# Weight tiles of 2048 columns in place of 1024, each split by one copy and one subtract

## The chip, the cores and the metric

The kernel runs on one core of a Trainium2 chip. The time is the device time of one execution in microseconds (us). Engines: TensorE (PE, with its weight load PEld) multiplies, VectorE (DVE) and ScalarE (ACT) work on tiles elementwise, GpSimd (POOL) does small helpers, SyncE (SP) issues most DMA transfers from DRAM.

## The reference

The program is a two-layer network on x of 256 tokens by 1024 features, all in float32. Each layer is: a feed-forward block, a mixer (short convolution, a gated recurrence, pooling), a cross attention to 256 memory rows, and a second feed-forward block; each is followed by a residual and a layer norm.

```python
def swiglu(x, w_gate, w_up, w_down):
    return (jax.nn.silu(x @ w_gate) * (x @ w_up)) @ w_down
# ffn1_gate, ffn1_up: (DEPTH, 1024, 2816); ffn1_down: (DEPTH, 2816, 1024); ffn2 alike
# w_in: (DEPTH, 1024, D_IN); w_out, ca_q, ca_k, ca_v, ca_o: (DEPTH, 1024, 1024)
```

Every weight is used by one product per layer, so all weights stream from DRAM once: 216 MB in one execution.

## The kernel before, in words

**Products in parts.** A float32 factor is written as the sum of two rounded parts, high and low (type fp32r). `split(hi, lo, src)` (lines 60 to 62) makes them: ScalarE copies src into hi (line 61, shown as CAST `whi<-raw` for weights), and VectorE subtracts hi from src into lo (line 62, `wlo<-raw,whi`). A product is then three matmuls: high by high, high by low and low by high (`mm_rows`, lines 129 to 132, all through line 105).

**Weight tiles.** `load` (lines 64 to 93) brings a weight matrix in steps of 128 partitions by 2048 float32 numbers. Each step is two tiles of 1024 columns: two `raw` tiles filled by one DMA of 512 KB each, two `whi` and two `wlo` tiles, and two calls of `split`. The pool holds 6 `raw`, 8 `whi` and 8 `wlo` buffers, which are handed out in turn. A buffer can be filled again when the last reader of the tile in it is done. At the start, the very first weights come with `fine=True` in pieces of 512 columns. `Weights.at(k, cols)` finds the high and low slices of a block k.

**Feed-forward.** `ffn` (from line 400) walks over six column chunks of gate and up (five of 512 and one of 256). The chunk `first` makes gate and up products of its own; the middle ones are either `hidden`, which multiplies the whole gate chunk and then the whole up chunk, or `by_seven` (lines 568 to 652). Each chunk's activations are turned by DMA and VectorE (`turn`), and the down products of a chunk (`both`, tags `dn`, two slabs of 2048 columns) follow one or two chunks later. In layer 0's first ffn only chunk 4 goes by seven products; in the other three ffns chunks 2 and 4 do, so there are seven such chunks in all.

**by_seven.** Four blocks of weights (gate and up, upper and lower half of the features) are called w00, w01, w10 and w11. Instead of eight block products it makes seven, in this order: w00, w00+w01, w00+w11, w01+w11, w11, w10, w00+w10. The sums are made on VectorE in place (line 597). Each block is two tiles of 1024 columns: w00 in buffers spare0 and spare1, w01 in the buffers of the layer norm's parameters (lng, lnb), w11 in two `raw` buffers, w10 in spare2 and one `raw` buffer. Partial products lie in `sg` and `half` tiles (line 619).

**Order.** Apart from the program's first chunk, whose order is written by hand (line 494), a scheduler sets the order of instructions on each engine from the program's order, buffers and dependencies. Each engine then runs its own list strictly in order. The weight loads are issued on SP's queue.

**Other users.** `keys`, `values`, `mixer` and the attention call `load` for their weights in the same buffers; `finish` (line 303) does the layer norms and, in between, transposes h into xT (line 172), which again go through `split`.

Of the kernel before, what the change touches and what calls it, by code (L numbers as in the profile page):

```python
# [8 lines left out]
F32 = mybir.dt.float32  # L9
F32R = mybir.dt.float32r  # L10
U8 = mybir.dt.uint8
AF = mybir.ActivationFunctionType
ALU = mybir.AluOpType
# [4 lines left out]
P = 128  # L18
DEPTH = 2
SEQ = 256  # L20
DM = 1024
# [7 lines left out]
CHUNK = 512  # L29
# [17 lines left out]
def model(ctx: ExitStack, tc: tile.TileContext, t: dict, out: bass.AP):  # L47
    nc = tc.nc
    cst = ctx.enter_context(tc.tile_pool(name="cst", bufs=1))
    wp = ctx.enter_context(tc.tile_pool(name="wp", bufs=1))  # L50
# [9 lines left out]
    def split(hi, lo, src):  # L60
        nc.scalar.copy(hi, src)  # L61
        lows.append(nc.vector.tensor_tensor(lo, src, hi.bitcast(F32), op=ALU.subtract))  # L62

    def load(src, k0, nk, c0, ncol, fine=False):


        hi, lo, todo = [], [], []
        step = 2048 // ncol
        for a in range(k0, k0 + nk, step):
            half = step // 2  # L70
            raw = [
                wp.tile([P, 1024], F32, tag="raw", name="raw", bufs=6).rearrange("p (k c) -> p k c", c=ncol)
                for _ in range(2)
            ]
            part = 1 if fine else half
            for b in range(0, step, part):
                loads.append(nc.sync.dma_start(
                    raw[b // half][:, b % half : b % half + part, :],
                    src[(a + b) * P : (a + b + part) * P, c0 : c0 + ncol].rearrange("(k p) c -> p k c", p=P),
                ))  # L80
            for s in range(2):
                h = wp.tile([P, 1024], F32R, tag="whi", name="whi", bufs=8)
                w = wp.tile([P, 1024], F32R, tag="wlo", name="wlo", bufs=8)
                h = h.rearrange("p (k c) -> p k c", c=ncol)
                w = w.rearrange("p (k c) -> p k c", c=ncol)
                r = raw[s]
                if fine:
                    todo += [(h[:, b, :], w[:, b, :], r[:, b, :]) for b in range(half)]
                else:
                    split(h, w, r)  # L90
                hi.append(h)
                lo.append(w)
        return Weights(hi, lo, half, todo)

# [47 lines left out]
    h = [cst.tile([P, DM], F32, name=f"h{i}") for i in range(NT)]  # L144
# [36 lines left out]


    def load_memory(mp, behind):
        m = [
            mp.tile([P, DM], F32, tag=f"spare{n}", name="m", bufs=1).rearrange("p (k b j) -> p k b j", k=4, j=32)
            for n in range(2)
        ]
        with tc.issue_after(behind.ins):
            for n in range(2):
                for a in range(4):  # L190
                    for k in range(4):
                        c = (4 * n + k) * P + a * 32
                        nc.gpsimd.dma_start(
                            m[n][a * 32 : a * 32 + 32, k],
                            t["mem"][0, :, c : c + 32].rearrange("(b i) j -> i b j", i=32),
                        )

        def later():
            for n in range(2):
                for k in range(0, 4, 2):  # L200
                    turned = mp.tile([P, 2, SEQ], F32, tag="up", name="turned")
                    nc.vector.transpose(
                        turned.rearrange("p k t -> p (k t)"), m[n][:, k : k + 2].rearrange("p k b j -> p (k b j)")
                    )
                    d = slice(4 * n + k, 4 * n + k + 2)
                    split(mTh[:, d, :], mTl[:, d, :], turned)

        return later
# [82 lines left out]


    def ln_params(l, n):
        g = wp.tile([P, DM], F32, tag="lng", name="lng")
        b = wp.tile([P, DM], F32, tag="lnb", name="lnb")
        nc.sync.dma_start(g, t["ln_g"][l, n : n + 1, :].to_broadcast([P, DM]))
        nc.sync.dma_start(b, t["ln_b"][l, n : n + 1, :].to_broadcast([P, DM]))
        return g, b
# [101 lines left out]
    def ffn(l, name, n, pend=None, last=False, early=None):  # L400
        gate, up, down = (t[f"{name}_{x}"][l] for x in ("gate", "up", "down"))
        with tc.tile_pool(name="ffn", bufs=2, reuse_waits="tile") as fp:
# [19 lines left out]
            def activations():  # L422
                return fp.tile([P, NT, CHUNK], F32, tag="sg", name="sg", bufs=1)
# [142 lines left out]
                return parts  # L566

            def by_seven(c0, bx):
                def rows_by_columns(r):
                    return r.rearrange("p (k c) -> p k c", c=CHUNK)  # L570

                def pieces(*tags):
                    return [
                        rows_by_columns(
                            (fp if "spare" in g else wp).tile([P, DM], F32, tag=g, name="raw", bufs=6 if g == "raw" else 1)
                        )
                        for g in tags
                    ]

                def block(m, j, to):  # L580
                    for i in range(2):
                        k = 4 * j + 2 * i
                        loads.append(nc.sync.dma_start(
                            to[i], m[k * P : (k + 2) * P, c0 : c0 + CHUNK].rearrange("(k p) c -> p k c", p=P)
                        ))
                    return to

                w00 = block(gate, 0, pieces("spare0", "spare1"))
                w01 = block(up, 0, pieces("lng", "lnb"))
                w11 = block(up, 1, pieces("raw", "raw"))  # L590
                w10 = block(gate, 1, pieces("spare2", "raw"))

                def parts_of(r, plus=None):
                    hi, lo = [], []
                    for i in range(2):
                        if plus is not None:
                            nc.vector.tensor_tensor(r[i], r[i], plus[i], op=ALU.add)  # L597
                        h = wp.tile([P, 1024], F32R, tag="whi", name="whi", bufs=8)
                        w = wp.tile([P, 1024], F32R, tag="wlo", name="wlo", bufs=8)
                        h, w = (rows_by_columns(x) for x in (h, w))  # L600
                        split(h, w, r[i])
                        hi.append(h)
                        lo.append(w)
                    return Weights(hi, lo, 2, [])

                def part_of_x(i, j):
                    d = slice(4 * j, 4 * j + 4)
# [7 lines left out]
                def half_sum():  # L615
                    return fp.tile([P, 4, P], F32, tag="up", name="half").rearrange("p k t -> p (k t)")
# [4 lines left out]
                s = activations()  # L621
                g = [s[:, i, :] for i in range(NT)]
# [9 lines left out]
                f = half_sum()  # L632
# [47 lines left out]
            bx = []  # L680

            if early is None:
                d = [fp.tile([P, DM], F32, tag=f"spare{n}", name="quarters", bufs=1) for n in range(2)]
            else:
                d = [wp.tile([P, DM], F32, tag=g, name="quarters") for g in ("lng", "lnb")]
            q = [d[n // 2].rearrange("p (n k t) -> p n k t", n=2, t=P)[:, n % 2] for n in range(4)]

            chunks = [(c, min(CHUNK, DFF - c)) for c in range(0, DFF, CHUNK)]

# [22 lines left out]
            for c, (c0, ncol) in enumerate(chunks):  # L712
                if not c:
                    acts.append(first())
                    ys = [[acc((P, 512), "dn") for _ in range(2)] for _ in range(NT)]
                elif c in sevens:
                    left = by_seven(c0, bx)
                else:
                    if c in (1, 2) and early is not None:
                        acts.append(hidden(c0, aside))  # L720
                    else:
                        acts.append(hidden(c0) if ncol == CHUNK else last_hidden(c0))
                if c == 1 and early is None:
                    bx.extend(blocks_of_x())
                if c == max(sevens) + 1:
                    gb = ln_params(l, n)
                if c == 1 and early is not None:

                    with tc.issue_after(loads[-1].ins):
                        rest = early(fp)  # L730
                if c == 2 and early is not None:
                    with tc.issue_after(lows[-1].ins):
                        rest[0]()
                if c > 0:
                    if c > 1:
                        both(c - 2, 1)
                    if c in sevens:
                        acts.append(left())
                    if c < len(chunks) - 1:
                        both(c - 1, 0)  # L740
# [442 lines left out]
    def beginnings(op):  # L1183
        parameters, made = small_parameters(op)
        return parameters, load_memory(op, made)
# [35 lines left out]
```

## Time and profile before

| what | value |
|---|---|
| median of 3 runs | 1070.54 us (1070.43 to 1071.01) |
| span of the profiled execution | 1068.8 us |
| PE busy | 1059.3 us, 99% |
| PEld busy | 937.7 us, 88% |
| DVE busy, instructions | 946.3 us, 89%, 1318 |
| ACT busy, instructions | 642.4 us, 60%, 916 |
| read from HBM | 216.15 MB |

The span runs from the first to the last instruction of the profiled execution; the profile gives the execution no other time of its own, and the median of the runs is 1.7 us above the span. Busy time of an engine leaves out register, branch and DMA-issuing instructions. The busy shares are averages over the whole span. The granted TensorE clock was 0.998 of full speed over the span. Rows of instruction groups read: line, engine, operation, output<-inputs, shapes, count, then busy us and mean ns of one, then the idle time of the engine before them and what ended it. Rows of single instructions read: start in us from the span's start, length, engine, line, operation, tiles, count in a row, and in brackets the idle time before it.

### The profile page before, as it was taken

The numbers are of one execution on the slowest core, as the hardware profiler recorded it, in microseconds if no ns is written. First come the engines' busy times: TensorE is split into PE (matmuls) and PEld (weight loads), VectorE is DVE, ScalarE is ACT, GpSimd is POOL, SyncE is SP. The second block draws the span as 40 slices with busy tenths as digits, with TensorE's granted clock in tenths as the row PEclk, the third lists the DMA queues.
The fourth block names the chain that finished last, engine by engine and source line by source line (L and its number), as shares of the span: only waits on it lengthen the run. The fifth ranks groups of instructions, "written<-read, shape, count | busy, mean of one in ns | idle before, by whom it ended". The sixth has DMA issues, their size and how long they took to land.

```text
span 1068.8 us, 16312 instructions
## 1 busy us (share of the span) xinstructions
PE 1059.3 (99%) x5966; PEld 937.7 (88%) x5966; DVE 946.3 (89%) x1318; ACT 642.4 (60%) x916; POOL 66.4 (6%) x114
## 2 busy tenths in 40 slices
PE   9999999999999999999999999999999999999997
PEld 7888888889899888888888888888898998888886
DVE  6977997998988799999799999788989787999996
ACT  7555664666557565656575557566764665656660
POOL 9700001000000000000000000010000000000000
PEclk9999999999999999999999999999999999999999
DMA  9997484755574575848675865856536665759461
GB/s 362 262 307 256 129 288 165 249 176 174 170 278 167 178 252 194 290 167 218 238 272 184 256 254 183 290 179 216 196 126 213 241 227 181 257 156 334 134 223 40
DMA packets 130895, 231.90 MB, mean 217 GB/s; under 512 B 9408, under 2 KB 48608, under 8 KB 130816
## 3 DMA queue, kind: packets, MB, share of 16 engines
q1 hardware_dynamic: 129024, 228.49, 64.8%
q0 software_dynamic: 1216, 1.20, 0.5%
q8 instruction: 47, 0.77, 0.3%
q10 hardware_dynamic: 576, 1.18, 0.3%
q14 instruction: 32, 0.26, 0.1%
HBM read 216.15 MB, written 1.05 MB: 203 GB/s over the span
## 4 chain that ended last, share of the span: by engine, by line
PE 99%; DMA 0%; DVE 0%; issue 0%; DVEq 0%
PE acc L105 65%; PE dn L105 31%; PE acc L172 1%; PE dn L923 1%; PE dn L982 0%; DMA h<-in_x_dram 0%; PE acc L491 0%; PE dn L981 0%; PE dn L971 0%; PE acc L1047 0%; PE dn L888 0%; DVE h L358 0%; DVE h L353 0%; PE dn L472 0%; DVE st L338 0%
## 5 line engine op out<-in xcount | busy, mean ns | idle before, releaser
L61 ACT CAST whi<-raw 128x1024 fp32r<-128x1024 f32 (+1 forms) x438 | 442.9, 1042 | 197.5 <-DVE raw L597 54.9
L62 DVE TENSOR_TENSOR wlo<-raw,whi 128x1024 fp32r<-128x1024 f32 (+1 forms) x438 | 515.7, 1209 | 32.6 <-ACT whi L61 29.0
L105 PE MATMUL acc<-whi,xT 128*128 128x512 f32 x1032 | 312.9, 380 | 0.0
L105 PEld LDWEIGHTS acc<-whi,xT 128*128 128x128 f32 x1032 | 195.1, 189 | 27.5
L105 PE MATMUL acc<-wlo,xT 128*128 128x512 f32 x516 | 195.6, 379 | 0.0
L105 PE MATMUL acc<-xT,whi 128*128 128x512 f32 x576 | 142.3, 383 | 0.2
L105 PE MATMUL dn<-whi,ah 128*128 128x512 f32 x346 | 131.5, 380 | 0.0
L105 PE MATMUL dn<-wlo,ah 128*128 128x512 f32 x346 | 131.2, 379 | 0.0
L105 PE MATMUL dn<-whi,al 128*128 128x512 f32 x346 | 131.2, 379 | 0.0
L105 PEld LDWEIGHTS acc<-xT,whi 128*128 128x128 f32 x576 | 104.0, 190 | 12.5 <-ACT whi L61 0.7
L105 PEld LDWEIGHTS acc<-wlo,xT 128*128 128x128 f32 x516 | 97.5, 189 | 13.8
L105 PE MATMUL dn<-whi,xT 128*128 128x512 f32 x288 | 87.9, 381 | 0.0
L105 PEld LDWEIGHTS acc<-xT,wlo 128*128 128x128 f32 x576 | 75.5, 191 | 3.9
L105 PE MATMUL acc<-xT,wlo 128*128 128x256 f32 x576 | 75.9, 275 | 0.0
L105 PEld LDWEIGHTS dn<-whi,al 128*128 128x128 f32 x346 | 65.4, 189 | 9.2
L105 PEld LDWEIGHTS dn<-wlo,ah 128*128 128x128 f32 x346 | 65.4, 189 | 9.2
L105 PEld LDWEIGHTS dn<-whi,ah 128*128 128x128 f32 x346 | 65.4, 189 | 9.1
L350 POOL TENSOR_TENSOR rs<-rs,nhalf 128x1 f32<-128x1 f32 x16 | 14.9, 930 | 833.6 <-DVE rs L346 598.1
L597 DVE TENSOR_TENSOR raw<-raw 128x1024 f32<-128x1024 f32 x56 | 66.2, 1217 | 0.4
L105 PEld LDWEIGHTS dn<-whi,xT 128*128 128x128 f32 x288 | 54.4, 189 | 7.7 <-DVE xT L62 0.3
L105 PE MATMUL dn<-wlo,xT 128*128 128x512 f32 x144 | 54.6, 379 | 0.0
L332 DVE SCALAR_TENSOR_TENSOR h<-h,dn 128x512 f32<-128x512 f32 x31 | 21.2, 683 | 32.9 <-PE dn L105 32.9
(234 smaller groups left out, 1277.5 us busy)
## 6 DMA issues: line engine op xcount, KB each, us to landing
raw<-in_ffn_up_dram SPq DMA_DIRECT2D x88, 512.0 KB, 5.3
raw<-in_ffn_down_dram SPq DMA_DIRECT2D x88, 512.0 KB, 6.6
raw<-in_ffn_gate_dram SPq DMA_DIRECT2D x84, 512.0 KB, 5.1
raw<-in_w_in_dram SPq DMA_DIRECT2D x48, 512.0 KB, 4.7
dealt<-sg SPq DMA_DIRECT2D x80, 128.0 KB, 4.7
raw<-in_ca_k_dram SPq DMA_DIRECT2D x16, 512.0 KB, 4.9
raw<-in_w_out_dram SPq DMA_DIRECT2D x16, 512.0 KB, 4.5
raw<-in_ca_v_dram SPq DMA_DIRECT2D x16, 512.0 KB, 5.3
```

Source lines behind the costliest of these rows:

```text
L61: nc.scalar.copy(hi, src)
L62: lows.append(nc.vector.tensor_tensor(lo, src, hi.bitcast(F32), op=ALU.subtract))
L105: nc.tensor.matmul(o, w, x, start=start, stop=stop)
L172: nc.tensor.transpose(pt[:, k, :], src[:, (4 * j + k) * P : (4 * j + k + 1) * P], unit)
L332: nc.vector.scalar_tensor_tensor(v, v, ALPHA / scale, sums(y[i][n]), op0=ALU.mult, op1=ALU.add, accum_out=None if junk is None else st[:, ...
L350: nc.gpsimd.tensor_tensor(rs, rs, nhalf[:, 0:1], op=ALU.pow)
L597: nc.vector.tensor_tensor(r[i], r[i], plus[i], op=ALU.add)
L923: nc.tensor.matmul(o[g, hh, :], kc[:, hh, g], x, start=True, stop=True)
```

## The change

A tile of weights is 2048 columns wide: `raw` has 3 buffers in place of 6, `whi` and `wlo` 4 in place of 8, which are the same bytes. `load` calls `split` once per tile in place of twice, so one ScalarE copy and one VectorE subtract treat 128x2048 numbers. The loads themselves stay 512 KB each, two per tile. In `by_seven`, w00, w11 and w10 taken alone are split by one instruction pair as well; the sums stay additions of 1024 columns and splits of 1024 columns, but both additions now stand ahead of both splits, and the high and low tiles are one 2048 buffer each. w10 takes a whole `raw` buffer, so spare2 isn't used for it; spare0 and spare1 become one tile, as do lng and lnb.

```diff
+    def wide(kind, tag, n, ncol):
+        return wp.tile([P, 2048], kind, tag=tag, name=tag, bufs=n).rearrange("p (k c) -> p k c", c=ncol)
+
     def load(src, k0, nk, c0, ncol, fine=False):
         hi, lo, todo = [], [], []
         step = 2048 // ncol
         for a in range(k0, k0 + nk, step):
-            half = step // 2
-            raw = [
-                wp.tile([P, 1024], F32, tag="raw", name="raw", bufs=6).rearrange("p (k c) -> p k c", c=ncol)
-                for _ in range(2)
-            ]
-            part = 1 if fine else half
+            r = wide(F32, "raw", 3, ncol)
+            part = 1 if fine else step // 2
             for b in range(0, step, part):
                 loads.append(nc.sync.dma_start(
-                    raw[b // half][:, b % half : b % half + part, :],
+                    r[:, b : b + part, :],
                     src[(a + b) * P : (a + b + part) * P, c0 : c0 + ncol].rearrange("(k p) c -> p k c", p=P),
                 ))
-            for s in range(2):
-                h = wp.tile([P, 1024], F32R, tag="whi", name="whi", bufs=8)
-                w = wp.tile([P, 1024], F32R, tag="wlo", name="wlo", bufs=8)
...
-                    split(h, w, r)
-                hi.append(h)
-                lo.append(w)
-        return Weights(hi, lo, half, todo)
+            h, w = wide(F32R, "whi", 4, ncol), wide(F32R, "wlo", 4, ncol)
+            if fine:
+                todo += [(h[:, b, :], w[:, b, :], r[:, b, :]) for b in range(step)]
+            else:
+                split(h, w, r)
+            hi.append(h)
+            lo.append(w)
+        return Weights(hi, lo, step, todo)
...
     def ln_params(l, n):
-        g = wp.tile([P, DM], F32, tag="lng", name="lng")
-        b = wp.tile([P, DM], F32, tag="lnb", name="lnb")
+        both = wp.tile([P, 2, DM], F32, tag="ln", name="ln")
+        g, b = both[:, 0, :], both[:, 1, :]
...
-                w00 = block(gate, 0, pieces("spare0", "spare1"))
-                w01 = block(up, 0, pieces("lng", "lnb"))
-                w11 = block(up, 1, pieces("raw", "raw"))
-                w10 = block(gate, 1, pieces("spare2", "raw"))
+                w00 = block(gate, 0, fp, "spare")
+                w01 = block(up, 0, wp, "ln")
+                w11 = block(up, 1, wp, "raw", 3)
+                w10 = block(gate, 1, wp, "raw", 3)
 
                 def parts_of(r, plus=None):
-                    hi, lo = [], []
-                    for i in range(2):
-                        if plus is not None:
-                            nc.vector.tensor_tensor(r[i], r[i], plus[i], op=ALU.add)
-                        h = wp.tile([P, 1024], F32R, tag="whi", name="whi", bufs=8)
-                        w = wp.tile([P, 1024], F32R, tag="wlo", name="wlo", bufs=8)
-                        h, w = (rows_by_columns(x) for x in (h, w))
-                        split(h, w, r[i])
-                        hi.append(h)
-                        lo.append(w)
-                    return Weights(hi, lo, 2, [])
+                    h, w = wide(F32R, "whi", 4, CHUNK), wide(F32R, "wlo", 4, CHUNK)
+                    if plus is None:
+                        split(h, w, r)
+                    else:
+                        pairs = [slice(0, 2), slice(2, 4)]
+                        for k in pairs:
+                            nc.vector.tensor_tensor(r[:, k], r[:, k], plus[:, k], op=ALU.add)
+                        for k in pairs:
+                            split(h[:, k], w[:, k], r[:, k])
+                    return Weights([h], [w], 4, [])
```

The remaining lines of the diff rename the buffers in `load_memory` and in the tiles called quarters accordingly.

More of the change, by code (lines that the diff above doesn't have):

```diff
@@ L69, in load @@
         for a in range(k0, k0 + nk, step):
-            half = step // 2
-            raw = [
-                wp.tile([P, 1024], F32, tag="raw", name="raw", bufs=6).rearrange("p (k c) -> p k c", c=ncol)
-                for _ in range(2)
-            ]
-            part = 1 if fine else half
+            r = wide(F32, "raw", 3, ncol)
+            part = 1 if fine else step // 2
             for b in range(0, step, part):
                 loads.append(nc.sync.dma_start(
-                    raw[b // half][:, b % half : b % half + part, :],
+                    r[:, b : b + part, :],
                     src[(a + b) * P : (a + b + part) * P, c0 : c0 + ncol].rearrange("(k p) c -> p k c", p=P),
                 ))
-            for s in range(2):
-                h = wp.tile([P, 1024], F32R, tag="whi", name="whi", bufs=8)
-                w = wp.tile([P, 1024], F32R, tag="wlo", name="wlo", bufs=8)
[L84 to L89, printed above, removed]
-                    split(h, w, r)
-                hi.append(h)
-                lo.append(w)
-        return Weights(hi, lo, half, todo)
+            h, w = wide(F32R, "whi", 4, ncol), wide(F32R, "wlo", 4, ncol)
[6 more added lines that the diff above has]
+        return Weights(hi, lo, step, todo)
     def halves(a):
@@ L183, in load_memory @@
     def load_memory(mp, behind):
[L184 to L187, printed above, removed]
+        m = mp.tile([P, 2 * DM], F32, tag="spare", name="m", bufs=1)
+        m = m.rearrange("p (n k b j) -> p n k b j", n=2, k=4, j=32)
         with tc.issue_after(behind.ins):
@@ L193, in load_memory @@
                         nc.gpsimd.dma_start(
-                            m[n][a * 32 : a * 32 + 32, k],
+                            m[a * 32 : a * 32 + 32, n, k],
                             t["mem"][0, :, c : c + 32].rearrange("(b i) j -> i b j", i=32),
@@ L202, in later @@
                     nc.vector.transpose(
-                        turned.rearrange("p k t -> p (k t)"), m[n][:, k : k + 2].rearrange("p k b j -> p (k b j)")
+                        turned.rearrange("p k t -> p (k t)"), m[:, n, k : k + 2].rearrange("p k b j -> p (k b j)")
                     )
@@ L568, in by_seven, with block @@
             def by_seven(c0, bx):
[L569 to L580, printed above, removed]
+                def block(m, j, pool, tag, n=1):
+                    to = pool.tile([P, 2048], F32, tag=tag, name="raw", bufs=n).rearrange("p (k c) -> p k c", c=CHUNK)
                     for i in range(2):
@@ L583, in block @@
                         loads.append(nc.sync.dma_start(
-                            to[i], m[k * P : (k + 2) * P, c0 : c0 + CHUNK].rearrange("(k p) c -> p k c", p=P)
-                        ))
-                    return to
-                w00 = block(gate, 0, pieces("spare0", "spare1"))
-                w01 = block(up, 0, pieces("lng", "lnb"))
-                w11 = block(up, 1, pieces("raw", "raw"))
-                w10 = block(gate, 1, pieces("spare2", "raw"))
+                            to[:, 2 * i : 2 * i + 2, :],
+                            m[k * P : (k + 2) * P, c0 : c0 + CHUNK].rearrange("(k p) c -> p k c", p=P),
+                        ))
+                    return to
+                w00 = block(gate, 0, fp, "spare")
+                w01 = block(up, 0, wp, "ln")
+                w11 = block(up, 1, wp, "raw", 3)
+                w10 = block(gate, 1, wp, "raw", 3)
                 def parts_of(r, plus=None):
-                    hi, lo = [], []
-                    for i in range(2):
-                        if plus is not None:
-                            nc.vector.tensor_tensor(r[i], r[i], plus[i], op=ALU.add)
-                        h = wp.tile([P, 1024], F32R, tag="whi", name="whi", bufs=8)
-                        w = wp.tile([P, 1024], F32R, tag="wlo", name="wlo", bufs=8)
-                        h, w = (rows_by_columns(x) for x in (h, w))
-                        split(h, w, r[i])
-                        hi.append(h)
-                        lo.append(w)
-                    return Weights(hi, lo, 2, [])
+                    h, w = wide(F32R, "whi", 4, CHUNK), wide(F32R, "wlo", 4, CHUNK)
[8 more added lines that the diff above has]
+                    return Weights([h], [w], 4, [])
                 def part_of_x(i, j):
@@ L682, in ffn @@
             if early is None:
-                d = [fp.tile([P, DM], F32, tag=f"spare{n}", name="quarters", bufs=1) for n in range(2)]
+                d = fp.tile([P, 2 * DM], F32, tag="spare", name="quarters", bufs=1)
             else:
-                d = [wp.tile([P, DM], F32, tag=g, name="quarters") for g in ("lng", "lnb")]
-            q = [d[n // 2].rearrange("p (n k t) -> p n k t", n=2, t=P)[:, n % 2] for n in range(4)]
+                d = wp.tile([P, 2, DM], F32, tag="ln", name="quarters").rearrange("p n c -> p (n c)")
+            d = d.rearrange("p (n k t) -> p n k t", n=4, t=P)
+            q = [d[:, n] for n in range(4)]
             chunks = [(c, min(CHUNK, DFF - c)) for c in range(0, DFF, CHUNK)]
```

## The prediction

> **What bounds the kernel now.** I read the page first, then the chain that ended last, the groups with each shape apart, windows of single stages, and single instructions. The page's head, busy rows, clock and shares of the chain:
>
> ```profile
> span 1068.8 us, 16312 instructions
> ...
> PE 1059.3 (99%) x5966; PEld 937.7 (88%) x5966; DVE 946.3 (89%) x1318; ACT 642.4 (60%) x916; POOL 66.4 (6%) x114
> ...
> PEclk9999999999999999999999999999999999999999
> ...
> PE 99%; DMA 0%; DVE 0%; issue 0%; DVEq 0%
> PE acc L105 65%; PE dn L105 31%; PE acc L172 1%; PE dn L923 1%; PE dn L982 0%; DMA h<-in_x_dram 0%; PE acc L491 0%; PE dn L981 0%; PE dn L971 0%; PE acc L1047 0%; PE dn L888 0%; DVE h L358 0%; DVE h L353 0%; PE dn L472 0%; DVE st L338 0%
> ```
>
> TensorE sets the time. It is idle 1068.8 - 1059.3 = 9.5 us, and the chain runs through it for 99%. Two pieces of the chain in order of time (start, length, matmuls):
>
> ```profile
> 18.18 31.08 PE acc L105 x144
> 54.44 20.72 PE acc L105 x96
> ```
>
> 31.08 / 144 and 20.72 / 96 are both 216 ns a matmul: long runs without any stall. So a change that leaves the matmuls alone can win next to nothing; it can lose wherever a weight tile comes late. Whether one does hangs on VectorE, shown by two windows (length; then busy us and instructions of PE, PEld, DVE, ACT):
>
> ```profile
> 98.00:140.00 42.00, 42.00 (x196) 36.80 (x195) 40.95 (x45) 25.33 (x27) 0.00 (x0) 1.00 0.46 149
> ...
> 412.00:433.00 21.00, 21.00 (x99) 18.36 (x98) 21.00 (x25) 12.53 (x14) 0.00 (x0) 1.00 0.59 168
> ```
>
> Around a chunk done by seven products (by_seven) VectorE is as full as TensorE: 40.95 of 42 and 21.00 of 21 us. A delay there isn't made up.
>
> **Price of one instruction.** Groups with shapes apart (busy, mean ns; idle before and who ended it), ScalarE, then VectorE:
>
> ```profile
> L61 ACT CAST whi<-raw 128x1024 fp32r<-128x1024 f32 x430 | 438.2, 1049 | 197.2 <-DVE raw L597 54.9 <-PE dn L105 53.5 <-PE acc L105 35.5
> ...
> L61 ACT CAST whi<-raw 128x512 fp32r<-128x512 f32 x8 | 4.7, 624 | 0.3 <-DMA raw<-in_ffn_gate_dram 0.3
> ```
>
> ```profile
> L62 DVE TENSOR_TENSOR wlo<-raw,whi 128x1024 fp32r<-128x1024 f32 x430 | 510.4, 1219 | 32.5 <-ACT whi L61 29.0 <-PE acc L105 1.9
> ...
> L62 DVE TENSOR_TENSOR wlo<-raw,whi 128x512 fp32r<-128x512 f32 x8 | 5.4, 709 | 0.1
> ```
>
> 512 more columns cost 425 ns of copy and 510 ns of subtract, so I estimate 1049 + 850 = 1.90 us and 1219 + 1020 = 2.24 us for 2048 columns. Two subtracts back to back start 1.13 us apart (row at 425.98 below: 2.35 - 1.22), copies 0.95 us (row at 430.18: six spacings in 6.74 - 1.05); a merged pair thus occupies about 2.15 and 1.80 us in place of 2.26 and 1.90. The built program has 187 fewer instructions on each engine: 187 x 0.11 = 21 us saved on VectorE, 187 x 0.10 = 19 us on ScalarE, all beside TensorE.
>
> **The change part by part.** Matmuls, loads (number, size, queue), blockwise adds and bytes of buffers stay: nothing by themselves; if their cover went, it would show in the terms below.
>
> What costs is the grain. A 2048 buffer is free only when the readers of both its halves are done, so the copy into it starts one half later; and VectorE, which had its first half after 1.05 us of copy, waits 1.90.
>
> (a) *Start.* Row of ScalarE: a half of the first up tile comes at 14.03; below it TensorE's first low product of that tile.
>
> ```profile
> 14.03 1.04 ACT L61 CAST whi<-raw 128x1024 fp32r<-128x1024 f32 x1 [0.16 <-DMA raw<-in_ffn_up_dram]
> ```
>
> ```profile
> 18.23 0.38 PE L105 MATMUL acc<-wlo,xT 128*128 128x512 f32 x1
> ```
>
> Merged: 14.03 + 1.90 + 2.24 = 18.17 against 18.23. I take 0.1 (0 to 1.1, one subtract spacing).
>
> (b) *First by_seven of layer 0.* Copies of w00 now wait for both halves of an up tile:
>
> ```profile
> 98.67 1.05 ACT L61 CAST whi<-raw 128x1024 fp32r<-128x1024 f32 x1 [0.69 <-PE acc L105]
> 101.26 1.05 ACT L61 CAST whi<-raw 128x1024 fp32r<-128x1024 f32 x1 [1.54 <-PE acc L105]
> ```
>
> ```profile
> 132.36 1.21 DVE L62 TENSOR_TENSOR wlo<-raw,whi 128x1024 fp32r<-128x1024 f32 x1
> ```
>
> ```profile
> 134.89 0.38 PE L105 MATMUL dn<-wlo,ah 128*128 128x512 f32 x1
> ```
>
> The first copy moves from 98.67 to 101.26, 2.59 us later, and lasts 0.85 us longer, so VectorE falls 3.4 us behind in a full stage. The down tile behind the seven products ends at 133.57 with both halves; as one tile it is needed at 134.89, a reserve of 1.3. 3.4 - 1.3 = 2.1, less 0.1 saved on merges: 2.0 (0 to 3.4).
>
> (c) *First chunk of the three later ffns.* In the built order one product of the up tile stands three places into the chunk, where its neighbours are still gate products.
>
> ```profile
> 364.46 0.38 PE L105 MATMUL dn<-whi,xT 128*128 128x512 f32 x1
> ...
> 368.57 0.59 PE L105 MATMUL acc<-whi,xT 128*128 128x512 f32 x2
> ```
>
> ```profile
> 366.18 1.06 ACT L61 CAST xT<-acc 128x512 fp32r<-128x512 f32 x2
> 367.13 3.89 ACT L61 CAST whi<-raw 128x1024 fp32r<-128x1024 f32 x4
> ```
>
> The buffer of the last gate tile comes free whole at 364.7: its copy until 366.7, two copies for xT (0.95), then the up tile until 369.6, with TensorE there at 368.57: 1.0 each (0 to 1.9, the whole copy), 3.0. Everything behind it on the queue waits too; the transposes of h1 ahead of it do not.
>
> (d) *The second chunk's by_seven in the same three ffns.* VectorE, then ScalarE, then TensorE's low products of the last run, (w00+w10), and of the down tile behind it:
>
> ```profile
> 425.98 2.35 DVE L62 TENSOR_TENSOR wlo<-raw,whi 128x1024 fp32r<-128x1024 f32 x2
> ...
> 431.27 3.50 DVE L62 TENSOR_TENSOR wlo<-raw,whi 128x1024 fp32r<-128x1024 f32 x3
> ```
>
> ```profile
> 430.18 6.74 ACT L61 CAST whi<-raw 128x1024 fp32r<-128x1024 f32 x7 [5.42 <-DVE raw L597]
> ```
>
> ```profile
> 431.39 0.38 PE L105 MATMUL acc<-wlo,xT 128*128 128x512 f32 x1
> ...
> 432.69 0.38 PE L105 MATMUL acc<-wlo,xT 128*128 128x512 f32 x1
> ...
> 433.98 0.38 PE L105 MATMUL dn<-wlo,ah 128*128 128x512 f32 x1
> ```
>
> Before, the second low half ends at 431.27 + 1.22 = 432.49, 0.20 us ahead of its use. After, both adds stand ahead of the first low half, so that one ends at 432.4 and is needed at 431.39: 1.0 late. Then the order is the down tile (2.15, to 434.6) and the second half (to 435.7), while TensorE has ten down products moved between the halves. It reaches their first low product 1.3 + 0.2 us after the late start, at 433.9; 0.8 more, and with the second half hidden behind the ten, 2.0 with the switch. I add 0.8 for VectorE's late entry by mechanism (b) (bounds 0 and 3.4, nearer 0 because transposes and subtracts fill that wait here): 2.8 each (0.8 to 5.4), 8.4.
>
> (e) *The fifth chunk's by_seven in these ffns* has the reserve of (b), but keeps some earlier work ahead: 1.1 each (0 to 2.0), 3.3.
>
> (f) *Six entries of mixer, its column blocks and attention* (three a layer) start with a new tile. One such place:
>
> ```profile
> 189.10 2.35 DVE L62 TENSOR_TENSOR wlo<-raw,whi 128x1024 fp32r<-128x1024 f32 x2
> ```
>
> ```profile
> 190.32 1.05 PE L105 MATMUL acc<-xT,wlo 128*128 128x256 f32 x8
> ```
>
> A low half ends at 190.32, inside the run that reads its tile. I take 0.5 each between 0 and one subtract spacing, 1.13: 3.0 (0 to 6.8).
>
> Sum: 0.1 + 2.0 + 3.0 + 8.4 + 3.3 + 3.0 = 19.8 us of stalls. The profiled span is 1068.8 and the median 1070.54, 1.7 outside the span: 1068.8 + 19.8 + 1.7 = 1090.3, say 1090.
>
> The Trainium skill, "Perfetto Trace Analysis", section "Optimizing Scalar/DVE Operations", sets two rules side by side: larger operations improve throughput if the engine is saturated, and where Scalar and Vector aren't saturated but cause bubbles elsewhere, smaller instructions let work complete sooner. By the second the sum stands; by the first it would be near 1070. The trace has VectorE saturated in the seven-product stages and not over the span, so both speak here.
>
> **Rivals.** *No change, 1070.5.* The 21 us that VectorE saves pay for the late grain, and each tile is still there in time. For it: no wait of TensorE shows before, and most tiles have microseconds of reserve. Against: savings of 0.11 us a pair come spread out, while a reserve of 0.20 us meets a delay of 1 to 2.
>
> *Faster, 1069 to 1070.* Larger operations relieve the saturated VectorE, and TensorE's small bubbles go. It decides if part of the 9.5 us idle are waits for low tiles. Against: runs at 216 ns a matmul, and 0% of the chain on VectorE; at most 1.5 us. This is the first rule of that page of the Trainium skill ("Perfetto Trace Analysis", same section) at work.
>
> *Slower still, 1103.* w11 and w10 now hold two of three raw buffers during a by_seven, where before they held three of six halves; the next slab's load starts only when w11's last subtract is done. Seven stages late by a load's order, taken as another 1.9 us each (one copy), add 13: 1090 + 13. For it: VectorE full at 412 to 433; against: the third buffer still takes the next down tile early.
>
> **How the numbers follow.** About 0.2% (2.1 us) is what a measurement of this kernel can tell from none. Forecast 0.65, slower still 0.20, no change 0.12, faster 0.03. The likeliest is 1090, its own range 1078 to 1098: terms (b) to (f) at half, and at 1.4 times. For 8 in 10 the range goes from 1073 (just above the no-change case, which with the faster one holds 0.15) to 1105 (which takes in the slower one). Slower by over 0.2%: 0.65 + 0.20 = 0.85; within: 0.12; faster: 0.03.
>
> **What would show it.** Right: VectorE's wlo<-raw,whi with 128x2048 at 2.2 us and ScalarE's at 1.9; busy of both down by some 20 us; TensorE idle up from 9.5 to about 29, in gaps of 1 to 3 us at the places of (b) to (f), ended by L62 or L61; matmuls elsewhere still 216 ns. Wrong: runs unbroken at those places (no change), gaps ended by a load from DRAM (slower still), or a 2048 instruction that costs more than twice a 1024 one.

## Result and profile after

The changed kernel takes 1109.09 us in the median (1108.23 to 1109.99) against 1070.76 us for the kernel before: a ratio of 1.036, 95% interval 1.034 to 1.037, or 38.3 us more. Forecast were 1090 us and a range up to 1105. The direction was right; the size was half of what came.

The head of the page after, with the shares of the chain that ended last:

```profile
span 1107.6 us, 15623 instructions
...
PE 1072.7 (97%) x5966; PEld 936.8 (85%) x5966; DVE 933.8 (84%) x1131; ACT 619.3 (56%) x729; POOL 62.4 (6%) x114
...
PE 49%; DVE 28%; issue 9%; ACT 8%; DMA 6%; SPq 1%; DVEq 0%; ACTq 0%
```

The matmuls are the same 5966, and VectorE and ScalarE have 187 instructions fewer each, but the chain now runs through TensorE for only 49% of the span: 28% of it is VectorE, 8% ScalarE, 6% loads. The page's PE busy rises from 1059.3 to 1072.7 us for the same matmuls, since their ends are modelled in the profile, so stalls are better read from the starts. Groups with shapes apart:

```profile
L62 DVE TENSOR_TENSOR wlo<-raw,whi 128x2048 fp32r<-128x2048 f32 x187 | 426.5, 2287 | 98.1 <-ACT whi L61 97.3
L61 ACT CAST whi<-raw 128x2048 fp32r<-128x2048 f32 x187 | 354.0, 1908 | 139.8 <-DMA raw<-in_ffn_up_dram 30.0 <-PE dn L99 23.9 <-DMA raw<-in_ffn_gate_dram 19.6
```

One instruction costs what was estimated: 2.29 us (2.24) and 1.91 us (1.90). VectorE's busy time fell by 12.5 us (21 were estimated), ScalarE's by 23.1 (19). But VectorE now waits 97.3 us for ScalarE's long copies, where it waited 29.0 before, and ScalarE's copies wait 67.6 us for the three weight matrices of the feed-forward (30.0, 20.1 and 17.5), where it was 38.5 before (13.6, 4.6 and 20.3).

For every pair of neighbouring matmuls I took the time between their starts beyond the median of that shape, and added it up by place, over the kernel before (us; the stages are cut at the same matmuls; "three" or "two" are the number of places; the prediction's second and fifth chunk are the kernel's chunks 2 and 4, counted from 0). A table column comes from one profiled execution; e1's was 1.5 us above its median.

| place | changed | halves on wide tiles (e1) | only raw wide (e9) | only high/low wide (e10) | forecast |
|---|---|---|---|---|---|
| start (to 18 us) | 1.8 | 0.3 | 1.0 | 0.5 | 0.1 |
| first by_seven and its down products | 2.4 | 1.7 | 0.1 | -0.1 | 2.0 |
| mixer, two | 5.2 | 1.8 | 0.0 | 2.3 | with next |
| attention, two | 7.0 | 0.9 | 0.0 | 0.9 | 3.0 |
| first chunk, three | 4.1 | 0.7 | 0.0 | 0.7 | 3.0 |
| second chunk's by_seven, three | 12.7 | 12.9 | 3.1 | 4.7 | 8.4 |
| fifth chunk's by_seven, three | 5.3 | 4.1 | 0.0 | 0.7 | 3.3 |
| everything | 38.8 | 22.0 | 4.1 | 9.3 | 19.8 |

The first row can hardly be an effect of the change: the kernels of this study start with 2.7 to 4.7 us of such time in no order, and two versions below with the same instructions at the start (e2, e14) have 2.8 and 2.9, as the kernel before has. What sets it isn't shown.

### The profile page after: what moved, and what is told of

Read it like the earlier page. It is cut to its first block, busy times and chain, and to the rows that moved or that the text cites. A ratio compares the mean times of both kernels' runs of the same rounds, so it can differ in the third digit from the quotient of the medians.

```text
span 1107.6 us, 15623 instructions
## 1 busy us (share of the span) xinstructions
PE 1072.7 (97%) x5966; PEld 936.8 (85%) x5966; DVE 933.8 (84%) x1131; ACT 619.3 (56%) x729; POOL 62.4 (6%) x114
## 3 DMA queue, kind: packets, MB, share of 16 engines
HBM read 216.15 MB, written 1.05 MB: 196 GB/s over the span
## 4 chain that ended last, share of the span: by engine, by line
PE 49%; DVE 28%; issue 9%; ACT 8%; DMA 6%; SPq 1%; DVEq 0%; ACTq 0%
PE acc L99 27%; PE dn L99 19%; DVE wlo L62 15%; ACT whi L61 6%; DVE raw L583 4%; DMA raw<-in_ffn_down_dram 2%; DMA raw<-in_ffn_up_dram 1%; DVE half L601 1%; DVE sg L432 1%; DMA raw<-in_ca_q_dram 1%; DVE square L445 1%; DMA dealt<-sg 1%; PE acc L166 1%; DVE sg L601 1%; DVE sums L120 1%
## 5 line engine op out<-in xcount | busy, mean ns | idle before, releaser
L62 DVE TENSOR_TENSOR wlo<-raw,whi 128x2048 fp32r<-128x2048 f32 (+2 forms) x251 | 497.2, 1997 | 98.4 <-ACT whi L61 97.6
L61 ACT CAST whi<-raw 128x2048 fp32r<-128x2048 f32 (+2 forms) x251 | 415.0, 1675 | 247.8 <-DVE raw L583 98.7
L99 PE MATMUL dn<-whi,ah 128*128 128x512 f32 x346 | 129.0, 382 | 6.8 <-ACT whi L61 6.8
L99 PEld LDWEIGHTS dn<-whi,ah 128*128 128x128 f32 x346 | 64.9, 189 | 17.5 <-ACT whi L61 8.9
L99 PE MATMUL acc<-wlo,kTh 128*128 128x512 f32 x112 | 42.7, 381 | 0.2
```

What stands on the lines that cost most here:

```text
L99: nc.tensor.matmul(o, w, x, start=start, stop=stop)
```

## Two causes: grain of the buffers, length of the instructions

Two theories stood against each other. *Grain*: a wide buffer is free only when both halves have been read, so copies and loads start late, whatever the size of the instructions. *Length*: a 1.9 us copy and a 2.3 us subtract bring the low part late and hold up what is queued behind them. The first runs tell them apart.

**e1: wide tiles, instructions of 1024 columns.**

```diff
-                split(h, w, r)
+                for b in range(0, step, step // 2):
+                    split(*(v[:, b : b + step // 2, :] for v in (h, w, r)))
```

and in by_seven each half is added and split in turn.

> Tiles of 2048 columns as in the changed kernel, but every split is made of two copies and two subtracts of 1024 columns, and in by_seven an addition stands ahead of its own split, as before the change. Theory G (grain: a buffer of 2048 columns is free only when all of it has been read, so copies and loads start late): most of the 38 us stay, 1095 to 1109 us, with TensorE gaps still ended by L61. Theory L (length: a copy of 1.9 us and a subtract of 2.2 us bring the low part late and hold up what is queued behind them): nearly all goes, 1071 to 1077 us, gaps of TensorE as before the change.

Measured: 1091.15 us, ratio 1.018 (1.016 to 1.020). Neither theory has it all: 20.2 of the 38.3 us stay with the wide tiles alone, 18 go with the long instructions. Of the 20.2, some 4.5 come from matmuls at half clock (427 ns apart in place of 216; last section), which the changed kernel, with a granted clock of 0.998 to 0.999, doesn't have behind its stalls. For the changed kernel itself I therefore estimate 16 us for the tiles and 22 for the length.

**e9: as e1, with high and low tiles narrow again (8 of 1024); e10: the kernel before, with only high and low tiles wide (4 of 2048).**

```diff
-            h, w = wide(F32R, "whi", 4, ncol), wide(F32R, "wlo", 4, ncol)
...
+            for b in range(0, step, half):
+                h, w = narrow("whi", ncol), narrow("wlo", ncol)
...
```

> As e1_halves, but the high and low tiles are 8 of 1024 columns again; only the raw tiles are 2048 wide, 3 in all, and w10 takes a whole one. Theory R (of the grain only the raw buffers count: loads wait for a whole tile's subtract and come late): the same time as e1_halves within 4 us. Theory G with the high and low tiles as its place: within 3 us of 1070.8. Theory L: within 3 us of 1070.8 too, and e1_halves with it.

> The kernel before with high and low tiles of 2048 columns, 4 each, filled by instructions of 1024 columns; raw tiles stay 6 of 1024. Theory R: within 3 us of 1070.8. Theory G with the high and low tiles as its place: the same as e1_halves within 4 us. Theory L: within 3 us of 1070.8.

Measured: e9 1074.25 us, ratio 1.003 (1.002 to 1.004), so 3.3 us; e10 1079.29 us, ratio 1.008 (1.006 to 1.009), so 8.3 us. Theory R falls as a sole cause, and so does one place alone: 3.3 + 8.3 = 11.6, and both together 20.2. About half of this surplus of 8.6 is e1's half clock.

**e2: the changed kernel with by_seven alone in halves; e3: e1 with by_seven alone whole.**

```diff
-                    if plus is None:
-                        split(h, w, r)
-                    else:
-                        pairs = [slice(0, 2), slice(2, 4)]
-                        for k in pairs:
-                            nc.vector.tensor_tensor(r[:, k], r[:, k], plus[:, k], op=ALU.add)
-                        for k in pairs:
-                            split(h[:, k], w[:, k], r[:, k])
+                    for k in (slice(0, 2), slice(2, 4)):
+                        if plus is not None:
+                            nc.vector.tensor_tensor(r[:, k], r[:, k], plus[:, k], op=ALU.add)
+                        split(h[:, k], w[:, k], r[:, k])
```

> The changed kernel with by_seven alone back at instructions of 1024 columns, an addition ahead of its own split. If by_seven's own whole splits and its order of additions make half of the loss, as the prediction's terms (b), (d) and (e) have it (13.7 of 19.8 us), about 1085 us; if the loss comes from load's instructions everywhere, 1100 us or more.

> Wide tiles with load's splits in halves of 1024 columns, and only by_seven as in the changed kernel: whole splits, both additions ahead of both splits. If whole splits in by_seven cost by themselves, as the prediction's (d) has it with the additions first: 1097 us or more. If not, as e2_load_whole with the time of the changed kernel suggests: within 3 us of e1_halves' 1091.

Measured: e2 1109.09 us, ratio 1.035 (1.034 to 1.037); e3 1087.76 us, ratio 1.016 (1.014 to 1.017). Beside loads in halves, whole splits inside by_seven and both additions ahead of them cost nothing: e3 is 3.4 us below e1, and e1 loses about as much at half clock, which e3 (0.998 to 0.999) doesn't have.

That e2 has the time of the changed kernel to the hundredth is chance. Its runs go from 1106.58 to 1110.34 us with granted clocks from 0.995 down to 0.991, and in its trace 3.0 us are matmuls at half clock. Between starts, by_seven in halves takes about 4 us off the changed kernel: 2.4 becomes 1.3 at the first by_seven, 12.7 becomes 11 at the second chunk's without the half clock, 5.3 becomes 3.6 at the fifth's. So beside long loads the whole splits do cost something, but the second chunk's loss is mostly not theirs.

The table's 12.7 and 12.9 for the second chunk are alike by chance too: e1's holds some 5 us of half clock, and e3, with a full clock, has 7.9. So about 8 of the 12.7 are grain, and the rest came with the length of the loads' instructions and of by_seven's.

**Is grain the same as fewer buffers? e11, e12, e13: the kernel before, all tiles narrow, with 7 high and low buffers in place of 8, with 5 raw in place of 6, or with both.**

```diff
...
-                h = wp.tile([P, 1024], F32R, tag="whi", name="whi", bufs=8)
+                h = wp.tile([P, 1024], F32R, tag="whi", name="whi", bufs=7)
...
```

> The kernel before with 7 buffers of 1024 columns for high and for low tiles in place of 8, nothing else. Theory G says that a wide tile acts like one half-tile fewer, since half of a freed tile waits for its other half: the same as e10_hilo_wide, 1079 us, within 4. If wide tiles hurt by the order that they give the instructions instead: 1071 to 1074 us.

> The kernel before with 5 raw buffers of 1024 columns in place of 6, high and low tiles 8 of 1024. Theory G, a wide tile acts like one half-tile fewer: as e9_raw_wide, 1074 us, within 3. With e11_seven_bufs (14.4 us over before) and e12_seven_five (23.1 over before) it also says whether the two narrowings add: if they do, 1079.5 us.

> The kernel before with 7 buffers for high and for low tiles and 5 for raw tiles, all of 1024 columns. Theory G: as e1_halves, 1091 us, within 5, more than the sum of the two narrowings alone (3.3 and 8.3 us). If the two add up: 1080 to 1084 us. If the count of buffers doesn't matter: 1071 to 1074 us.

Measured: e11 1085.16 us (1.014; 1.012 to 1.015), e13 1075.04 us (1.004; 1.003 to 1.006), e12 1093.78 us (1.022; 1.020 to 1.023). A kernel with no long instruction and no wide tile loses 23 us as soon as one half-tile of each pool is missing. This is close to e1's 20. It is more than the sum, 14.5 + 4.5 = 19, but in e12's trace 22 matmuls behind its stalls run at half clock, 4.6 us, and in e11's none there, so the surplus is the clock's. For the raw tiles the equation holds (4.5 against 3.3); for the high and low tiles a missing half costs more (14.5) than the wide grain (8.3), so it is a likeness and no identity. The eight high and low buffers were just enough.

One rival stays open here. With other buffers the scheduler also orders the instructions otherwise: e13 has TensorE's 5966 matmuls in the order of before, but VectorE's instructions differ at 260 of 1318 places, and e11's at 836. What a missing buffer costs by itself and what the new order costs isn't told apart.

How the grain gets to TensorE is seen in the changed kernel's stage ahead of a second chunk's by_seven. SP's issues of loads:

```profile
388.56 0.88 SPq L565 DMA_DIRECT2D raw<-in_ffn_up_dram  x2
398.24 0.88 SPq L76 DMA_DIRECT2D raw<-in_ffn_up_dram  x2
```

SP issues nothing for 8.8 us. The second pair of loads goes into the buffer of the raw tile three before it, whose subtract ends at 398.22, whole:

```profile
395.93 2.29 DVE L62 TENSOR_TENSOR wlo<-raw,whi 128x2048 fp32r<-128x2048 f32 x1
```

A wait at this place is not new: the kernel before has 6.7 us there (377.85 to 384.52), and e1 7.1. Counted from the same matmul, the pair goes out 2.0 us later than before, and 2.3 us later in e1, which has only the wide tiles. ScalarE, and then VectorE, of the changed kernel in the next microseconds:

```profile
403.46 1.90 ACT L61 CAST whi<-raw 128x2048 fp32r<-128x2048 f32 x1 [2.39 <-DMA raw<-in_ffn_up_dram]
408.50 1.92 ACT L61 CAST whi<-raw 128x2048 fp32r<-128x2048 f32 x1 [3.13 <-DMA raw<-in_ffn_down_dram]
```

```profile
405.40 2.29 DVE L62 TENSOR_TENSOR wlo<-raw,whi 128x2048 fp32r<-128x2048 f32 x1 [0.90 <-ACT whi L61]
410.45 2.29 DVE L62 TENSOR_TENSOR wlo<-raw,whi 128x2048 fp32r<-128x2048 f32 x1 [2.76 <-ACT whi L61]
...
416.71 2.29 DVE L62 TENSOR_TENSOR wlo<-raw,whi 128x2048 fp32r<-128x2048 f32 x1 [1.36 <-ACT whi L61]
```

VectorE loses 0.90 + 2.76 + 1.36 = 5.0 us in this stage. The kernel before loses 1.05 us there, in one wait, and e1, with instructions of 1024 columns, 2.08 + 1.27 + 0.44 = 3.8:

```profile
398.83 1.23 DVE L62 TENSOR_TENSOR wlo<-raw,whi 128x1024 fp32r<-128x1024 f32 x1 [1.05 <-ACT whi L61]
```

```profile
401.05 1.23 DVE L62 TENSOR_TENSOR wlo<-raw,whi 128x1024 fp32r<-128x1024 f32 x1 [2.08 <-ACT whi L61]
...
404.76 1.29 DVE L62 TENSOR_TENSOR al<-square,ah 128x512 fp32r<-128x512 f32 x2 [1.27 <-ACT ah L61]
406.50 3.50 DVE L62 TENSOR_TENSOR wlo<-raw,whi 128x1024 fp32r<-128x1024 f32 x3 [0.44 <-ACT whi L61]
```

So most of the lateness is the grain's. The stage behind, by_seven itself, is the one that the prediction had shown with VectorE full (412 to 433). VectorE is full there in the changed kernel too and can't make the time up. TensorE pays at the end of by_seven, where the reserve was smallest:

```profile
441.52 0.48 PE L99 MATMUL acc<-wlo,xT 128*128 128x512 f32 x1 [0.84 <-DVE wlo L62]
...
444.40 0.48 PE L99 MATMUL acc<-whi,xT 128*128 128x512 f32 x1 [0.24 <-ACT whi L61]
446.20 1.13 PE L99 MATMUL dn<-whi,ah 128*128 128x512 f32 x4 [1.32 <-ACT whi L61]
...
448.92 0.48 PE L99 MATMUL dn<-wlo,ah 128*128 128x512 f32 x1 [0.29 <-DVE wlo L62]
```

(A wait's number is the idle time alone; between starts, the longest of them makes 1.58 us.) The prediction named the run of w00+w10 and the moved down products; what holds them longest is not a low tile, but the down tile's high copy, which ScalarE can only make behind the copy of w00+w10, and that one waits for VectorE's addition, until 443.31:

```profile
443.31 5.60 ACT L61 CAST whi<-raw 128x1024 fp32r<-128x1024 f32 x4 [6.94 <-DVE raw L583]
```

The row merges two copies of 1024 columns (1.04 us each) and two of 2048 (1.89 and 1.90). The down tile's is the second, from 444.26 to 446.15, so at this point the length of the copy adds to the grain.

## Where the length costs

**e5 and e6: in the changed kernel, whole splits with the copy alone, or the subtract alone, in two halves.**

```diff
+    def split_tile(hi, lo, src, copies=2, subtracts=1):
+        for a, b in zip(halves_of(hi, copies), halves_of(src, copies)):
+            nc.scalar.copy(a, b)
+        for a, b, c in zip(*(halves_of(v, subtracts) for v in (lo, src, hi))):
+            lows.append(nc.vector.tensor_tensor(a, b, c.bitcast(F32), op=ALU.subtract))
...
-                split(h, w, r)
+                split_tile(h, w, r)
```

This is e5; e6 has copies=1 and subtracts=2. halves_of cuts a tile into that many parts.

> The changed kernel, with the copy of each whole tile made as two of 1024 columns and the subtract left whole. e1_halves leaves some 18 us of the loss to the length of the instructions. If the long copy carries it (first chunks, where TensorE waits for a high tile): about 1098 us. If the long subtract carries it (the attention's and the mixer's small subtracts queued behind it): within 4 us of 1109.

> The changed kernel, with the subtract of each whole tile made as two of 1024 columns and the copy left whole. If the long subtract carries the length part: about 1095 us. If the long copy carries it: within 4 us of 1109. Both in part: about 1100 us.

Measured: e5 1101.50 us, ratio 1.029 (1.027 to 1.030); e6 1102.69 us, ratio 1.030 (1.028 to 1.032). They give back 7.6 and 6.4 of the 18 us; e6's trace has 2.7 us of matmuls at half clock and e5's none, so halved subtracts are worth nearer 9. Neither the copy nor the subtract is the culprit alone.

**e14: in the changed kernel the weights of mixer and attention in halves; e15: the complement, feed-forward and by_seven in halves.**

```diff
-    def load(src, k0, nk, c0, ncol, fine=False):
+    def load(src, k0, nk, c0, ncol, fine=False, whole=False):
...
-                split(h, w, r)
+                if whole:
+                    split(h, w, r)
+                else:
+                    for b in range(0, step, step // 2):
+                        split(*(v[:, b : b + step // 2, :] for v in (h, w, r)))
```

In e14 the calls of the feed-forward pass whole=True; in e15 the defaults are the other way round and by_seven is that of e1.

> The changed kernel, with the weights of mixer and attention (w_in, w_out, ca_*) split by two copies and two subtracts of 1024 columns on the same wide tiles; feed-forward and by_seven stay whole. In the changed kernel TensorE stands still 3.2 us longer per attention stage and 1.7 us longer per mixer than with halves everywhere, put down to small steps queued behind a 2.2 us subtract (theory Q). Q: 1109.1 - 2 x 3.2 - 2 x 1.7 = 1099 us, within 2.5. If those stalls come from the feed-forward before them (buffers, late loads): within 2.5 us of 1109.

> The complement of e14: feed-forward and by_seven split in halves of 1024 columns, mixer and attention whole, all on wide tiles. Q: e1_halves + 9.8 = 1101 us, within 3. If the stalls of mixer and attention come from the feed-forward: 1091 us, as e1_halves, within 3.

Measured: e14 1098.97 us, ratio 1.026 (1.025 to 1.028); e15 1098.02 us, ratio 1.025 (1.024 to 1.027). Theory Q gave 1099 and 1101; the second came 3 us lower, at the edge of its range. By the medians, long instructions in mixer and attention cost 10.1 us beside a long feed-forward (e14 against the changed kernel) and 6.9 beside one in halves (e15 against e1, which has more half clock). Between starts, mixer and attention lose 12.2 us in the changed kernel, 11.6 in e15, 3.8 in e14 and 2.7 in e1. So 8 to 9 us are made there, and not by the feed-forward ahead. The changed kernel's VectorE, ScalarE and TensorE at such a place in the attention:

```profile
340.01 0.42 DVE L120 TENSOR_TENSOR sums<-acc,sums 128x256 f32<-128x256 f32 x1
340.34 2.28 DVE L62 TENSOR_TENSOR wlo<-raw,whi 128x2048 fp32r<-128x2048 f32 x1
342.54 0.68 DVE L62 TENSOR_TENSOR qTl<-sums,qTh 128x512 fp32r<-128x512 f32 x1
```

```profile
340.46 0.62 ACT L61 CAST qTh<-sums 128x512 fp32r<-128x512 f32 x1 [0.60 <-DVE sums L120]
```

```profile
341.13 0.38 PE L99 MATMUL dn<-kTh,qTh 128*128 128x256 f32 x1 [0.86 <-ACT qTh L61]
...
343.28 0.38 PE L99 MATMUL dn<-kTh,qTl 128*128 128x256 f32 x1 [0.36 <-DVE qTl L62]
```

A sum of 0.42 us starts at 340.01, because a weight's subtract ran until then; the copy qTh waits for the sum and TensorE for qTh. Then the next weight's subtract of 2.28 us goes ahead of the 0.68 us subtract that makes qTl, and TensorE stands again. No weight tile is late here: small steps on the way to the next matmul are queued behind long ones.

## Why the prediction was half right

- *What bounds the kernel, and that nothing was to be won*: right. VectorE and ScalarE got 35.6 us of busy time less, and none of it came back as time.
- *Price of an instruction*: right for its length, 0.05 us off. The saving on VectorE was taken too high: two long subtracts start 2.20 us apart (4.49 - 2.29, row below), so a pair saves 0.06 and not 0.11 us.

```profile
399.34 4.49 DVE L62 TENSOR_TENSOR wlo<-raw,whi 128x2048 fp32r<-128x2048 f32 x2
```

- *(b)*: nearly right in size, 2.4 against 2.0, but in part by luck. At the down tile that the term names only 0.5 us is lost; 0.9 comes earlier, inside by_seven, and 1.2 later, in the down products 30 us behind, of which the term says nothing.
- *(c)*: right in place, a wait of 0.91 us for the up tile's high copy, and nearly in size: 4.1 against 3.0. Halves leave 0.7.
- *(d)*: right in place, 12.7 against 8.4. The reason given, both additions ahead of the first low half, is not the main one, since about 11 stay without it (e2). The entry, "0.8 for VectorE's late entry", is the part that was mis-sized: VectorE loses 5.0 us ahead of this by_seven in place of 1.05, behind raw tiles that come late, which the sum had left at nothing.
- *(e)*: 5.3 against 3.3. VectorE enters with one wait of 4.94 us (at 471.40), where the kernel before had three waits of 1.1 in all. So VectorE's late entry was priced too low here too; by_seven's own whole splits make 1.7 of the 5.3 (e2).
- *(f)*: the step that failed most, 12.2 against 3.0. "Six entries ... start with a new tile" priced a weight tile that arrives half a tile late. Only one entry a layer loses time that way, 0.8 us at the place that the prediction shows, and it does so with instructions in halves as well (e1). The rest is mostly small steps of mixer and attention behind long subtracts and copies, at several places inside a stage. That makes 9.2 of the 19.0 us missing between starts (38.8 - 19.8); (d) makes 4.3, (e) 2.0, the start 1.7, (c) 1.1, (b) 0.4, and 0.3 lie elsewhere.
- *The range*: all terms at half come to 1080.5, not to the 1078 that stands there. This did not decide anything, as the miss is on the other side.
- *The rivals*: "slower still" came nearest with 1103, but its mechanism, loads held up by w11 and w10 in two of three raw buffers, is worth 3.3 us alone (e9); with the wide high and low tiles it is more, 20.2 - 8.3 = 11.9 with e1's half clock in it. "No change" fell with the reserve of 0.20 us, as forecast.
- Of the two rules set side by side from the Trainium skill ("Perfetto Trace Analysis", section "Optimizing Scalar/DVE Operations"), the second held: with the same tiles, breaking the instructions up gains 18 us (1109.09 to 1091.15). The first did not even where VectorE was full, since TensorE had no stall there to give back.

## What to carry to other kernels

Where one engine runs without a gap, a merge of instructions on the engines that feed it has nothing to win, and the wider buffers take lookahead away, so price it by what waits behind the longest instruction on each queue and not by the time it saves. At equal bytes, buffers of double size are worth fewer buffers: test that first by taking a buffer away from the kernel as it is. Here one high and one low buffer of eight cost 14 us by themselves. Small steps on the critical path need short neighbours on their queue.

## What was not expected: the clock after two short stalls

In e1, TensorE's starts behind the stall in the second by_seven are 427 ns apart for some matmuls, not 216 as elsewhere. TensorE's rows of e1, and a window each before, in and after:

```profile
436.61 0.48 PE L100 MATMUL acc<-whi,xT 128*128 128x512 f32 x1 [1.73 <-ACT whi L61]
437.56 2.08 PE L100 MATMUL dn<-whi,ah 128*128 128x512 f32 x4 [0.46 <-ACT whi L61]
```

```profile
425.00:434.50 9.50, 9.50 (x45) 8.32 (x44) 9.50 (x13) 2.77 (x4) 0.00 (x0) 1.00 0.68 223
...
437.60:440.10 2.50, 2.50 (x6) 2.05 (x7) 2.50 (x3) 2.50 (x3) 0.00 (x0) 0.50 0.91 270
440.10:450.00 9.90, 9.90 (x46) 8.63 (x46) 8.54 (x11) 6.35 (x8) 0.00 (x0) 0.98 0.91 287
```

Two stalls of 1.73 and 0.46 us with one matmul between them, and the granted clock is 0.50 for some 2.5 us; at each of the three places of e1 some seven matmuls take 0.21 us longer, about 4.5 of its 12.9 us, and so part of why raw and high/low grain together cost more than their sum. e1's four runs had granted clocks from 0.993 to 0.997 and took 1093.0 to 1087.8 us, the shortest with the highest clock. It is not a matter of the stalls' length alone: in e2 the same two stalls (1.57 and 1.58 us more between starts) come three times, with the clock full behind the first and halved behind the third. Windows of e2 around them:

```profile
440.00:446.00 6.00, 3.27 (x15) 2.25 (x13) 6.00 (x6) 5.01 (x5) 0.00 (x0) 1.00 0.39 120
...
989.50:995.50 6.00, 6.00 (x15) 4.73 (x16) 6.00 (x5) 4.94 (x4) 0.00 (x0) 0.50 0.79 270
```

The Trainium skill, "TensorE: Matmul & The Clock Gate", section "HAM oscillation — how this bites in real kernels", gives as the rule that no idle gap should exceed about 3.4 us. These runs have the clock fall with gaps well below that. The same page says in "Part 1: The HAM clock gate (the "warmup" mystery)" that the window it watches runs free of the program, and e2's three places, equal in their stalls and unequal in their clock, agree with that; what the window adds up can't be told from these runs.
